# A hybrid DeltaNet / RWKV-7 / Mamba-2 layer on one core: a list scheduler inside the kernel orders every engine

## The chip, the core and the metric

The kernel runs on one core of a Trainium2 chip. The core has TensorE (PE, matrix products; its weight loads are shown apart as PEld), VectorE (DVE), ScalarE (ACT), GpSimd (POOL) and SyncE (SP), which each work through their own instructions in a fixed order, and DMA queues fed by SP and POOL. The metric is device microseconds (us) of one execution. The clock that TensorE is granted has two levels here, 2.4 GHz (shown as 1.00) and 1.2 GHz (0.50).

## What is computed

One residual layer over 16 meta frames and 1024 frames of width 1024. All three groups of heads read the same normalised input through one projection, and their outputs go through one output projection. Cut to what matters:

```python
hn = rms_norm(h, norm_pre)                       # (1040, 1024)
proj = einsum("bld,dp->blp", hn, w_in)           # 7832 columns, 61 tiles of 128 and 24 single ones
mixed = concat([
    gated_deltanet_group(p_a, ...),              # 6 heads of 128: conv, unit triangular solve per chunk, scan over chunks
    rwkv7_group(p_b, ...),                       # 8 heads of 64: token shift, low-rank decay, the same kind of solve and scan
    mamba2_group(p_c, ...)])                     # 12 heads of 64 in 4 groups: conv, chunked state-space scan
out = einsum("blm,md->bld", mixed, w_out)        # 2048 -> 1024
h = h + rms_norm(out, norm_post)
```

Each group multiplies its output by the silu of a gate, which is a tile of the projection of its own.

## The kernel before, in words

**Units.** The work is cut into twelve units: `unit_a` for each DeltaNet head (a0 to a5), `unit_b` for each pair of RWKV heads (b0 to b3), `unit_c` for each half of the Mamba heads (c0, c1), and at the end `unit_o`, the output projection. Each is a Python generator that writes instructions and yields at the points where it may be interrupted. `PLAN` gives the order in which units begin.

**Projections.** `proj` (L156) computes one 128-column tile of the input projection for all 1040 frames: in three pieces of about 350 frames, each 24 matmuls into one bank of PSUM (tile `pj`). Input and weights are split into a high and a low part in fp32r (`hh`, `hl` and the two halves of `w`), and for each of 8 blocks of the contraction three products are added: high weight by high input, high weight by low input, low weight by high input. `weights` (L142) brings a tile: SP loads it to `raw`, ACT writes the negated high part and the high part, and a DMA that POOL issues adds the raw weights to the negated part, which leaves the low part. 61 tiles make 4,392 matmuls. The output projection (tile `po`) has 768 more with 512 columns each, in the same fp32r form.

**Scans.** Everything else on PE (transposes, solves, the recurrences) is in plain fp32 with operands of 128, 64, 32 or 16 rows and columns; one such product stands in the trace as two matmul records. The solves of 32-blocks (`solve32`) run on DVE. A recurrence is a chain over chunks of PE, then DVE or ACT, then PE.

**Order.** `schedule` (L171) keeps a clock of its own from rough costs (`Meter`, L79): whenever the estimated time of a unit's next scan step has come, the step is written, otherwise the next products of a projection are ("fill"); a step counts as ready a margin after the last (`LATE`, `PIPE`, `SLOW`, and corrections to `lag`). Priorities (`PRI`, `EVA`, `CALM`) then let the framework's own scheduler move instructions. Units share two sets of PSUM banks ("lanes"); a third unit that scans shares a lane with another. 26 slots of SBUF (`NS`) are given to units by `safe`, so that a unit begins only when all can end. Projections that a unit needs late (its value, query and gate tiles) are put into a queue with a due time (`later`, `DUES`).

Of the kernel before, what the change touches and what calls it, by code (L numbers as in the profile page):

```python
# [7 lines left out]

# [6 lines left out]
F32 = mybir.dt.float32  # L15
# [6 lines left out]
D = 1024  # L22
KT = 8
# [5 lines left out]
FULL = ((0, 348), (348, 694), (694, 1040))  # L29
REAL = ((16, 358), (358, 700), (700, 1040))  # L30
# [12 lines left out]
XP = 500  # L43
# [6 lines left out]
SLOW = 1.0  # L50

PEAK = {"a": 7, "b": 12, "c": 14, "o": 24}
# [26 lines left out]
class Meter:  # L79


    def __init__(self, trunk, engine, fixed, each):
        self.trunk, self.engine, self.fixed, self.each = trunk, engine, fixed, each

    def __getattr__(self, name):
        op = getattr(self.engine, name)

        def call(out, *args, **kw):
            n = int(np.prod(out.shape[1:]))
            if name == "matmul":  # L90
                self.trunk.pe += n / 2400 if args[0].dtype == F32R else max(n, args[0].shape[-1]) / 600
            elif name == "transpose":
                self.trunk.pe += n / 1200
            elif not self.trunk.aside:
                self.trunk.lag += self.fixed + n * self.each
            return op(out, *args, **kw)  # L96

        return call


class Trunk:
    def __init__(self, tc, a):
        self.tc, self.nc, self.a = tc, tc.nc, a
        self.lane, self.pe, self.lag, self.aside = 0, 0.0, 0.0, False
        self.fetched, self.prefetch = {}, lambda i: None
        nc = tc.nc
        self.engines = tuple(Meter(self, e, f, n) for e, f, n in (
            (nc.vector, 0.25, 1 / 960), (nc.scalar, 0.3, 1 / 1200), (nc.tensor, 0, 0), (nc.gpsimd, 0.3, 1 / 500), (nc.sync, DMA, 0)))

    @contextmanager  # L110
    def off(self):

        self.aside = True
        yield
        self.aside = False
# [12 lines left out]
    def tmp2(self, name):  # L128
        return self.sm.tile([128, 2, 128], F32, tag="t2", name=name, bufs=1)
# [12 lines left out]
    def weights(self, i):  # L142
        nc = self.nc
        out = []
        for h in range(2):
            w = self.wp.tile([128, 2, 4, 128], F32R, tag="w", name=f"w{i}_{h}", bufs=NW)
            src = self.a["wt"][i][:, 4 * h: 4 * h + 4, :]
            raw = self.wp.tile([128, 4, 128], F32, tag="raw", name=f"wr{i}_{h}", bufs=NR)
# [7 lines left out]
    def proj(self, i, pieces, evac, halo=0):  # L156

        w = self.fetched.pop(i, None) or self.weights(i)
        for n, (a, b) in enumerate(pieces):
            a0 = max(a - halo, 0)  # L160
            p = self.pp.tile([128, 512], F32, tag="proj", name=f"pj{i}_{n}")
            for kt in range(KT):
                for m, (x, h) in enumerate(((0, self.hh), (0, self.hl), (1, self.hh))):
                    self.engines[2].matmul(p[:, : b - a0], w[kt // 4][:, x, kt % 4, :], h[:, kt, a0:b],
                                           start=(kt == 0 and m == 0), stop=(kt == KT - 1 and m == 2))
                    yield
            with self.tc.high_priority(EVA):
                evac(p, a, b, a - a0)
            if n == 0:
                self.prefetch(i)  # L170
# [33 lines left out]
    def setup(self):  # L204
# [15 lines left out]
        pk = cp.tile([128, sum(n for _, n in PACK)], F32, tag="pack", name="pack")  # L220
# [23 lines left out]
        for cc in XG:  # L244
# [5 lines left out]
            with self.tc.high_priority(XP):  # L250
# [116 lines left out]

    def unit_a(self, h):
# [34 lines left out]
        for cc, p in transposed(k, "akT", groups):  # L403
# [6 lines left out]
            yield PIPE  # L410
# [13 lines left out]
        for gi, cc in enumerate(groups):  # L424
# [7 lines left out]
            yield PIPE  # L432
# [12 lines left out]
        asked = self.later(h, self.conv(h, self.ctap_a[:, h, :], q, pieces=REAL), DUES[1])  # L445
        lb = self.one([128, 32, 32], f"alb{h}")
# [4 lines left out]
        yield 0.0  # L451
# [11 lines left out]
        for cc, p in transposed(v_, "avT", groups):  # L463
# [3 lines left out]
            yield PIPE  # L467
        yield from self.wait(asked)
        for cc, p in transposed(q, "aqT", groups[:2]):
# [3 lines left out]
            yield PIPE  # L473
        v.tensor_scalar(ss[:, 9:], ss[:, 9:], EPS, None, ADD)
        self.rsqrt(rs[:, 9:], ss[:, 9:], "a_q")
        self.lag = 0.0
        for gi, cc in enumerate(groups[:2]):
# [6 lines left out]
            yield PIPE  # L484
        yield 7
# [891 lines left out]
```

## Time and profile before

| | us |
|---|---|
| median of 3 runs | 1493.49 |
| lowest and highest | 1492.66, 1499.25 |
| the profiled execution | 1497.37 |
| its span, first to last instruction | 1495.2 |
| mean granted clock of TensorE in it (a share, 1 is full) | 0.956 |

The span is what the trace shows; the profiled execution's own time is 2.2 us longer, and 3.9 us above the median of the runs. PE is shown busy for 1439.9 us of the span, but its busy time overlaps from one matmul to the next, so the starts of successive matmuls are what tells how long each took.

### The profile page before, as it was taken

The numbers are of one execution on the slowest core, as the hardware profiler recorded it, in microseconds if no ns is written. First come the engines' busy times: TensorE is split into PE (matmuls) and PEld (weight loads), VectorE is DVE, ScalarE is ACT, GpSimd is POOL, SyncE is SP. The second block draws the span as 40 slices with busy tenths as digits, with TensorE's granted clock in tenths as the row PEclk, the third lists the DMA queues.
The fourth block names the chain that finished last, engine by engine and source line by source line (L and its number), as shares of the span: only waits on it lengthen the run. The fifth ranks groups of instructions, "written<-read, shape, count | busy, mean of one in ns | idle before, by whom it ended". The sixth has DMA issues, their size and how long they took to land.

```text
span 1495.2 us, 26098 instructions
## 1 busy us (share of the span) xinstructions
PE 1439.9 (96%) x9657; PEld 1274.6 (85%) x9657; DVE 954.8 (64%) x2688; ACT 707.2 (47%) x1936; POOL 173.4 (12%) x227
## 2 busy tenths in 40 slices
PE   5999999999999999999999999999999999999897
PEld 4999888888888789989888899889999988678686
DVE  6549485376768347869735787546588867542573
ACT  6455361345444364344746543544577255532530
POOL 2111000000001011111101111001132100200100
PEclk9999898799999799999979999889999999899999
DMA  7344332123223222434322244114534322553851
GB/s 225 87 114 85 81 61 58 43 62 93 51 46 75 67 71 72 116 65 103 76 86 57 62 85 96 29 43 99 118 97 105 71 58 59 171 162 89 259 191 57
DMA packets 120449, 136.28 MB, mean 91 GB/s; under 512 B 39867, under 2 KB 72379, under 8 KB 120323
## 3 DMA queue, kind: packets, MB, share of 16 engines
q1 hardware_dynamic: 102755, 102.64, 23.2%
q0 software_dynamic: 17568, 31.99, 12.7%
q8 instruction: 76, 1.25, 0.3%
q14 instruction: 50, 0.41, 0.1%
HBM read 116.99 MB, written 17.60 MB: 90 GB/s over the span
## 4 chain that ended last, share of the span: by engine, by line
PE 76%; issue 6%; DVE 6%; ACT 6%; DMA 5%; POOL 1%; SPq 0%; DVEq 0%; ACTq 0%; POOLq 0%
PE pj L96 41%; PE po L96 6%; PE bsi L96 5%; PE am L96 3%; PE bgr L96 2%; PE bu L96 2%; PE bm L96 1%; PE aops L96 1%; PE cdg L96 1%; PE ads L96 1%; PE bd L96 1%; PE av L96 1%; PE aks L96 1%; ACT buv L96 1%; DVE s_tmp L96 1%
## 5 line engine op out<-in xcount | busy, mean ns | idle before, releaser
L96 PE MATMUL pj<-hh,w 128*128 128x350 f32 (+8 forms) x2928 | 780.4, 340 | 4.5 <-DMA w<-in_wt_dram 2.7
L96 PEld LDWEIGHTS pj<-hh,w 128*128 128x128 f32 x2928 | 520.4, 193 | 19.4 <-DMA w<-in_wt_dram 2.9
L96 PE MATMUL pj<-hl,w 128*128 128x350 f32 (+8 forms) x1464 | 495.8, 339 | 0.0
L96 PEld LDWEIGHTS pj<-hl,w 128*128 128x128 f32 x1464 | 283.3, 193 | 6.1 <-issue 0.9
L152 POOL DMA_DIRECT2D w<-in_wt_dram x122 | 106.1, 870 | 903.5 <-ACT w L150 676.1
L150 ACT ACTIVATE w<-wr 128x512 fp32r<-128x512 f32 x122 | 76.6, 628 | 62.4 <-PE pj L96 61.2
L96 PE MATMUL po<-ow,omw 128*128 128x512 f32 x408 | 95.7, 395 | 4.1 <-ACT omw L1066 3.7
L96 PEld LDWEIGHTS po<-ow,omw 128*128 128x128 f32 x408 | 77.2, 191 | 22.6 <-ACT omw L1066 5.2
L96 PE MATMUL po<-ow,ome 128*128 128x512 f32 x360 | 92.0, 404 | 2.6 <-ACT ome L1066 1.2
L96 PEld LDWEIGHTS po<-ow,ome 128*128 128x128 f32 x360 | 67.8, 192 | 18.1 <-POOL ow L1049 2.1
L151 ACT CAST w<-wr 128x512 fp32r<-128x512 f32 x122 | 74.3, 609 | 0.1
L96 DVE TENSOR_TENSOR buv<-bu,b_ib 64x128 f32<-64x128 f32 x68 | 19.1, 281 | 81.2 <-PE bu L96 81.2
L96 PE MATMUL bsi<-buv,bgm 64*64 64x64 f32 (+1 forms) x528 | 62.1, 240 | 0.0
L96 DVE TENSOR_TENSOR alb<-alb,s_tmp 33x30 f32<-33x30 f32 (+9 forms) x180 | 56.7, 315 | 3.2 <-POOL alb L96 2.1
L96 DVE TENSOR_TENSOR s_tmp<-alb 33x30 f32<-33x30 f32 (+9 forms) x180 | 57.7, 320 | 1.1
L96 PEld LDWEIGHTS bsi<-buv,bgm 64*64 64x64 f32 (+1 forms) x528 | 42.6, 140 | 17.7 <-issue 3.2
L96 DVE SCALAR_TENSOR_TENSOR b_s<-bd,b_wc,b_s 64x64 f32<-64x64 f32 x120 | 33.9, 282 | 27.2 <-PE bd L96 23.1
L830 ACT COPY by<-bsi 64x128 f32<-64x128 f32 x64 | 16.8, 262 | 70.1 <-PE bsi L96 69.3
L96 ACT COPY b_x<-bsi 64x128 f32<-64x128 f32 x68 | 17.5, 258 | 62.7 <-PE bsi L96 62.4
L183 DVE SCALAR_TENSOR_TENSOR cbc<-pj,pack,cbc 128x346 f32<-128x346 f32 (+4 forms) x72 | 40.3, 567 | 9.8 <-ACT cbc L180 9.2
L1067 DVE TENSOR_TENSOR ome<-omre,ome 128x512 fp32r<-128x512 f32 (+2 forms) x40 | 22.9, 605 | 34.1 <-ACT ome L1066 34.0
L96 PE MATMUL bgr<-bar,bbk 64*128 64x128 f32 x272 | 42.4, 328 | 0.4 <-DVE bgm L96 0.4
(325 smaller groups left out, 2456.5 us busy)
## 6 DMA issues: line engine op xcount, KB each, us to landing
wr<-in_wt_dram SPq DMA_DIRECT2D x122, 256.0 KB, 3.4
w<-in_wt_dram POOLq DMA_DIRECT2D x122, 256.0 KB, 4.9
or<-in_w_out_dram SPq DMA_DIRECT2D x32, 256.0 KB, 4.2
omrw<-d_mix SPq DMA_DIRECT2D x32, 256.0 KB, 4.6
clt<-d_cs SPq DMA_DIRECT2D x24, 256.0 KB, 4.9
omre<-d_mix SPq DMA_DIRECT2D x24, 256.0 KB, 2.6
btw<-d_tw SPq DMA_DIRECT2D x8, 544.0 KB
x<-in_x_dram SPq DMA_DIRECT2D x8, 512.0 KB, 7.5
```

The source lines that it names most:

```text
L96: return op(out, *args, **kw)
L150: nc.scalar.activation(w[:, 1], raw, AF.Copy, scale=-1.0)
L151: nc.scalar.copy(w[:, 0], raw)
L152: nc.gpsimd.dma_start(w[:, 1], src, accum_op=ADD)
L183: nc.vector.scalar_tensor_tensor(acc[:, a + z: b], p[:, o + z - s: o + b - a - s], cw[:, 3 - s: 4 - s], acc[:, a + z: b], MUL, ADD)
L830: nc.scalar.copy(yt[hs[(c - 1) % 2], (c - 1) // 2, :], pq[64:128, 0:128])
L1067: nc.vector.tensor_tensor(t[:, 1], raw, t[:, 0].bitcast(F32), SUB)
```

## The change

The framework's ordering is replaced: each operation is recorded (`Scribe.write`) with the operations that it depends on and an estimate of its duration, and `schedule` emits, over all engines, whichever recorded instruction can start first, and ties each engine to that order. On PE it prefers a projection's matmul until 1.0 us of them have run (`BURST`), then emits the scan products that are ready, and keeps on while another becomes ready within 0.25 us (`JOIN`), first those of the same output tile. A decaying measure of the array's recent work (`heat`) forces projections when it is below `COLD`. Besides:

- within a piece of a projection, the 16 products with the high weights come first and the 8 with the low weights last; the next tile's weights are asked for after three matmuls of the first piece, before at its end
- gate tiles of `unit_a` and `unit_c` are computed in two pieces of 512 columns in place of three of 342
- the gates of a4 and a5 (`SOON`) are queued before the solve, in a slot more, in place of after it
- `PLAN` is another order; two units at most hold a lane, and a third waits with its scan
- `unit_o` loads one weight ahead in place of three, and each row block's final scaling is a task of its own

```diff
-LOOK, LATE, EVAC, DMA = 0.05, 0.3, 2.0, 5.0
-NOA = 3
-PIPE = 0.5
+NOA = 1
-PRI, EVA, CALM = 300, 700, 1500
+BURST, JOIN = 1.0, 0.25
+COOL, COLD = 3.0, 0.36
+LESS = {"scan": 0.0, "ev": 0.3, "ld": 0.5, "calm": 1.0, "off": 0.4}
+AHEAD = 8
-PLAN = "a0 b0 b1 b2 c0 b3 a1 a2 a3 c1 a4 a5"
+PLAN = "a0 b0 b1 a1 c0 b2 a2 c1 b3 a3 a4 a5"
+SOON = (4, 5)
...
-            for kt in range(KT):
-                for m, (x, h) in enumerate(((0, self.hh), (0, self.hl), (1, self.hh))):
-                    self.engines[2].matmul(p[:, : b - a0], w[kt // 4][:, x, kt % 4, :], h[:, kt, a0:b],
-                                           start=(kt == 0 and m == 0), stop=(kt == KT - 1 and m == 2))
-                    yield
+            steps = [(kt, 0, h) for kt in range(KT) for h in (self.hh, self.hl)] + [(kt, 1, self.hh) for kt in range(KT)]
+            for j, (kt, x, h) in enumerate(steps):
+                if n == 0 and j == 3:
+                    self.prefetch(i)
+                with self.of(cls="pj"):
+                    self.engines[2].matmul(p[:, : b - a0], w[kt // 4][:, x, kt % 4, :], h[:, kt, a0:b],
+                                           start=(j == 0), stop=(j == len(steps) - 1))
+                yield
...
+        return self.later(18 + h, self.proj(18 + h, HALF, gate), DUES[2])
...
+    def emit(self, i, start):
+        r = i.go()
...
+            self.tc.add_manual_dep(ins, was, mybir.DependencyInfo(mybir.DependencyClass.NoSync, mybir.DependencyReason.DATA), reason="order")
...
+                    if s["kind"] != "scan" or s["drop"] and s["want"] is None or s["task"].q["PE"] or s["task"].n > AHEAD:
+                        continue
+                    if s["on"] and not s["on"]["done"] or not safe(s):
+                        continue
+                    if s["lane"] is None:
+                        open_ = [g for g in range(len(GB)) if all(o["lane"] != g for o in active)]
+                        if not open_:
+                            continue
+                        s["lane"] = open_[0]
...
+                if e == "PE":
+                    now = self.free["PE"]
+                    pj = min((h for h in heads if h[2].cls == "pj"), key=lambda h: h[0], default=None)
+                    sc = [h for h in heads if h[2].cls != "pj"]
+                    sc = min(sc, key=lambda h: (h[0] > now + 0.02 if h[2].out == last else 1, h[0]), default=None)
+                    if pj is None or sc is None:
+                        pick = sc or pj
+                    elif heat * float(np.exp((self.seen_at - now) / COOL)) < COLD:
+                        pick = pj
+                    elif round_:
+                        pick = sc if sc[0] <= max(now + JOIN, pj[0]) else pj
+                    else:
+                        pick = sc if since >= BURST and sc[0] <= max(now + 0.03, pj[0]) or sc[0] < pj[0] - 0.3 else pj
+                else:
+                    first = min(h[0] for h in heads)
+                    pick = min((h for h in heads if h[0] <= first + 0.05), key=lambda h: h[1] + LESS[h[2].cls])
+                if best is None or pick[0] < best[0]:
+                    best = pick
```

## Rows read from the trace of the kernel before

**Rows 1.** The page: span, busy time by engine, and TensorE's granted clock in 40 slices.

```profile
span 1495.2 us, 26098 instructions
PE 1439.9 (96%) x9657; PEld 1274.6 (85%) x9657; DVE 954.8 (64%) x2688; ACT 707.2 (47%) x1936; POOL 173.4 (12%) x227
PEclk9999898799999799999979999889999999899999
```

**Rows 2.** Stretches: length; busy (count) of PE, PEld, DVE, ACT, POOL; granted clock; DMA.

```profile
104.80:108.20 3.40, 3.40 (x12) 3.40 (x12) 0.95 (x3) 2.07 (x3) 0.00 (x0) 0.50 0.12 39
...
248.10:282.30 34.20, 34.20 (x174) 25.87 (x175) 10.01 (x22) 6.08 (x17) 0.88 (x1) 0.50 0.07 12
493.90:511.00 17.10, 17.10 (x134) 14.34 (x130) 4.22 (x10) 5.72 (x15) 0.87 (x1) 0.50 0.16 45
760.10:777.20 17.10, 17.10 (x84) 13.59 (x82) 3.39 (x11) 5.28 (x15) 0.86 (x1) 0.50 0.15 32
...
1391.60:1395.00 3.40, 3.40 (x9) 2.61 (x9) 1.87 (x4) 1.94 (x4) 1.50 (x1) 0.50 0.96 280
```

**Rows 3.** The same view for tile pj alone: projections in two of these stretches.

```profile
248.10:282.30 34.20, 5.20 (x13) 3.43 (x14) 0.00 (x0) 0.00 (x0) 0.50 0.07 12
...
760.10:777.20 17.10, 6.20 (x13) 3.71 (x14) 0.00 (x0) 0.00 (x0) 0.50 0.15 32
```

**Rows 4.** PE in order of time at the lower clock: start, length of the group, operation.

```profile
264.86 0.47 PE L96 MATMUL bsi<-buv,bgm 64*64 64x64 f32 x2
265.26 0.80 PE L96 MATMUL bgr<-bar,bbk 64*128 64x128 f32 x4
265.99 0.47 PE L96 MATMUL bsi<-buv,bgm 64*64 64x64 f32 x2
```

**Rows 5.** PE in order of time at the full clock: one round between projections.

```profile
401.23 0.48 PE L96 MATMUL pj<-hh,w 128*128 128x346 f32 x2
401.55 0.32 PE L96 MATMUL pj<-hl,w 128*128 128x346 f32 x1
401.71 0.38 PE L96 MATMUL bd<-buv,bbt 128*128 128x128 f32 x2
402.02 0.45 PE L96 MATMUL bsi<-buv,bgm 128*64 128x64 f32 x4
402.39 0.58 PE L96 MATMUL pj<-hh,w 128*128 128x346 f32 x2
402.82 0.32 PE L96 MATMUL pj<-hl,w 128*128 128x346 f32 x1
```

**Rows 6.** PE in order of time: products of one form in a row.

```profile
1002.87 0.39 PE L96 MATMUL aops<-a_s,aq 128*128 128x128 f32 x2
1003.10 0.39 PE L96 MATMUL aops<-a_vn,aup 128*128 128x128 f32 x2
...
1202.58 1.14 PE L96 MATMUL am<-add,alo 64*64 64x64 f32 x16
```

**Rows 7.** PE in order of time: first and last round of the twelve units.

```profile
76.44 1.03 PE L96 MATMUL akT<-pack,ak 128*128 128x128 f32 x8
...
1321.58 1.09 PE L96 MATMUL aoT<-pack,avt 128*128 128x128 f32 x8 [1.52 <-DVE avt L96]
```

**Rows 8.** PE in order of time near the end: products with 512 columns.

```profile
1483.83 3.33 PE L96 MATMUL po<-ow,omw 128*128 128x512 f32 x14
```

**Rows 9.** Waits of PE: who waited for whom, us in total, times, longest.

```profile
PE xT L260 <- DVE x L255: 10.9, 1, 10.9
PE xT L260 <- DVE hl L264: 7.3, 5, 2.6
PE po L96 <- ACT omw L1066: 3.7, 1, 3.7
...
PE bvT L96 <- ACT buv L96: 2.2, 4, 1.1
...
PE aops L96 <- ACT avt L96: 1.6, 1, 1.6
```

More of the change, by code (lines that the diff above doesn't have):

```diff
@@ L76, in nt, with __init__ @@
     return NM if c == 0 else 128
-class Meter:
-    def __init__(self, trunk, engine, fixed, each):
-        self.trunk, self.engine, self.fixed, self.each = trunk, engine, fixed, each
+class Instr:
+    __slots__ = ("go", "eng", "deps", "cls", "step", "extra", "mode", "work", "lock", "took", "start", "done", "task", "out")
+class Task:
+    def __init__(self, name):
+        self.name, self.q = name, {e: [] for e in ENGINES}
+        self.n = 0
+ENGINES = ("PE", "ACT", "DVE", "POOL", "SP")
+SEES = {"PE": 0.055, "ACT": 0.035, "DVE": 0.035, "POOL": 0.075, "SP": 0.027}
@@ L85, in __getattr__, with __init__ @@
+class Scribe:
+    def __init__(self, trunk, key, engine):
+        self.trunk, self.key, self.engine = trunk, key, engine
     def __getattr__(self, name):
-        op = getattr(self.engine, name)
+        op, t = getattr(self.engine, name), self.trunk
+        if not t.writing:
+            return op
         def call(out, *args, **kw):
[L89 to L96, printed above, removed]
@@ L98, in __getattr__, with __init__, tile @@
-        return call
+            t.write(self.key, name, op, out, args, kw)
+        return call
+class Engines:
+    def __init__(self, trunk, nc):
+        self.vector, self.scalar, self.tensor = (Scribe(trunk, k, e) for k, e in (("DVE", nc.vector), ("ACT", nc.scalar), ("PE", nc.tensor)))
+        self.gpsimd, self.sync = Scribe(trunk, "POOL", nc.gpsimd), Scribe(trunk, "SP", nc.sync)
+class Pool:
+    def __init__(self, trunk, pool, bufs):
+        self.trunk, self.pool, self.bufs, self.made = trunk, pool, bufs, defaultdict(list)
+    def tile(self, shape, dt, tag, name, bufs=None):
+        t = self.pool.tile(shape, dt, tag=tag, name=name, **({} if bufs is None else {"bufs": bufs}))
+        if self.trunk.writing and tag != "s":
+            made, n = self.made[tag], bufs or self.bufs
+            key = t.tensor.name
+            if len(made) >= n:
+                old = made[-n]
+                self.trunk.born[key] = [a[2] for a in self.trunk.seen.get(old, ())]
+            made.append(key)
+        return t
@@ L110, in off, with of @@
-    @contextmanager
-    def off(self):
-        self.aside = True
-        yield
-        self.aside = False
+        self.nc = nc = Engines(self, tc.nc)
+        self.engines = (nc.vector, nc.scalar, nc.tensor, nc.gpsimd, nc.sync)
+        self.seen, self.born, self.task, self.cls = {}, {}, None, "scan"
+        self.before, self.free = {}, {e: 0.0 for e in ENGINES}
+        self.array, self.bus, self.held = None, 0.0, {"DVE": 0.0, "POOL": 0.0}
+    @contextmanager
+    def of(self, task=None, cls=None):
+        was = self.task, self.cls
+        self.task, self.cls = task or was[0], cls or was[1]
+        yield
+        self.task, self.cls = was
@@ new lines, in ready, with begins @@
+    def ready(self, i):
+        if i.start is None:
+            t = 0.0
+            for d in i.deps:
+                if d.done is None:
+                    return None
+                if not d.eng == i.eng == "PE":
+                    t = max(t, d.done + SEES[i.eng])
+            i.start = t
+        return i.start
+    def begins(self, i, t):
+        t = max(t, self.free[i.eng])
+        if i.lock:
+            other = self.held["POOL" if i.eng == "DVE" else "DVE"]
+            if t < other:
+                t = other + 0.02
+        return t
@@ new lines, in schedule @@
+        while True:
+            advance()
+            best = None
+            for e in ENGINES:
+                heads = []
+                for t in self.tasks:
+                    if t.q[e]:
+                        i = t.q[e][0]
+                        r = self.ready(i)
+                        if r is not None:
+                            heads.append((self.begins(i, r), r, i))
+                if not heads:
+                    continue
+                if e == "PE":
[9 more added lines that the diff above has]
+                        pick = sc if sc[0] <= max(now + JOIN, pj[0]) else pj
+                    else:
+                        pick = sc if since >= BURST and sc[0] <= max(now + 0.03, pj[0]) or sc[0] < pj[0] - 0.3 else pj
+                else:
+                    first = min(h[0] for h in heads)
+                    pick = min((h for h in heads if h[0] <= first + 0.05), key=lambda h: h[1] + LESS[h[2].cls])
+                if best is None or pick[0] < best[0]:
+                    best = pick
+            if best is None:
+                left = [t.name for t in self.tasks if t.n]
+                if left or units or active or self.queue or fill or out:
+                    raise ValueError(f"no part fits: {left} {units} {[(s['name'], s['has'], s['want'], s['drop'], s['kind']) for s in active]}")
+                break
+            start, _, i = best
+            if i.eng == "PE":
+                was = self.free["PE"]
+                if i.cls == "pj":
+                    since = since + i.step if not round_ else i.step
+                    round_ = False
+                else:
+                    round_ = True
+                last = i.out
+                heat = heat * float(np.exp((self.seen_at - start) / COOL)) + i.work / COOL
+                self.seen_at = start
+            self.emit(i, start)
+            self.tasks = [t for t in self.tasks if t.n or t is self.loader or t is self.mixer or any(t is s["task"] for s in active) or fill and (
+                t is fill.get("task") or fill.get("unit") and t is fill["unit"]["task"]) or planned and planned.get("unit") and t is planned["unit"]["task"]]
```

405 lines of the change are left out of this document (280 added, 125 removed).

## The prediction

> **What bounds the kernel now.** I read the page first. PE is shown busy 96% of the span, DVE 64%, ACT 47% [rows 1], so the question is what PE's time is made of. The waits of PE are next: the two largest are 18.2 us at the start, before any projection, and the others are single events of 0.5 to 4 us [rows 9]. So PE hardly ever waits for another engine, and a better order can't win much by removing waits. What it can win is that the same matmuls take less time each.
>
> PE's busy times overlap, so I took from the order in time the distance from each start to the next. A projection's product with 346 columns takes 0.16 us, also where `hh` and `hl` alternate [rows 5]; a product with 512 columns takes (3.33 - 0.38) / 13 = 0.227 us, where 0.38 is my reading of the last one's own length [rows 8]. An fp32 record of 128 by 128 takes 0.115 us (two from 1002.87 to 1003.10), one of 64 by 64 about 0.06 us ((1.14 - 0.2) / 15) [rows 6]. With such bare prices for every form, all matmuls together come to about 1267 us. From the first to the last start there are 1476 us. The 209 us between are what the change can reach, and two things make up most of it.
>
> The first is the clock. Of the stretches after the setup in which the granted clock is 0.50, the first begins at 104.8 us and the last at 1391.6; there are ten, of 126.5 us together [rows 2]. In nine of them PE is busy without a gap: 34.20 of 34.20 us in the longest. It isn't idling that they share, but what runs: 13 of 174 matmuls in that longest one are projections, 13 of 84 in another [rows 3]; the rest are small products. Everything takes about twice as long there: two 64-wide products and the change to the next form take 0.40 us [rows 4], and four with theirs 0.37 at the full clock [rows 5]. That fits a clock that falls with the amount of work in the array. The last stretch is another kind: it follows a wait of 3.7 us for `omw` [rows 2, 9].
>
> The second is changes of form. In one round at the full clock, bd takes 0.31 us where two bare records take 0.23, bsi 0.37 where four 64-wide ones take 0.24 [rows 6], and the two projections behind them 0.43 where they cost 0.32 [rows 5]: 0.08 + 0.13 + 0.11, so about 0.1 us a change. From the first to the last round I count 559 rounds of other matmuls, the first and the last of which are shown [rows 7], with 470 further changes of form inside them, and 558 runs of projections between, of which 405 have six products or fewer, that is under 1.0 us.
>
> **The change part by part.**
>
> *The clock (heat, COLD).* With little recent work in the array the scheduler now puts a projection ahead of a ready scan step. The projections aren't new work, only moved, and such stretches had one open: some of its products run in them [rows 3]. If the clock stayed up throughout, the 126.5 us would shrink to 63, a gain of 63; if it did nothing, 0. I take 46: nearer to the full gain because the condition that I read from rows 2 and 3 is the one that the rule acts on, and less than it because the wait at 1391 isn't touched, because slots can leave no projection open, and because each one put in costs changes of form.
>
> *Rounds (BURST, JOIN, outputs kept together).* Runs under 1.0 us are no longer chosen, unless the projection itself isn't ready. Where two units scan at once, their steps then meet in one round; where one scans alone, the round only comes later. Two rounds that meet save one change, 0.1 us. Bounds: none of the 405 meets, 0; all do, 41 us. I take half, 21, since mostly two units scan. In rounds, the rule of the last output tile keeps records of one tile together, where rows 4 show bsi and bgr cutting into each other every two to four records; of 470 changes I let 50 go, 5 us (bounds 0 and 15). Together 26.
>
> *Gate tiles in two pieces.* Three pieces of 342 are 72 products of 0.157 us (the 346-column price less 4 columns), 11.3 us; two of 512 are 48 of 0.227, 10.9 us. Over 12 tiles that is 5 us, and fewer evacuations on ACT and DVE, which have room. The Trainium skill ("TensorE: Matmul & The Clock Gate", Back-to-back issue gap) puts a product at columns / 2.4 GHz plus 2.5 ns: by that 10.44 and 10.36 us, an estimate of 1 us over all twelve, since the columns are the same. The rows are 12 ns above it for either width, so the number of products does count here, and the rows decide.
>
> *Low weights last, weights asked for earlier.* The low half is ready after the negated copy and POOL's DMA; now it is needed 16 products (2.5 us) into a tile. But PE's waits for `w` are below those of rows 9 but one of 2.7 us. Taken at 0; bounds 0 and 3. The cover is that weights of the next tile are fetched during a whole tile; if a tile runs with no scans between, it lasts 72 x 0.16 = 11.5 us, still enough.
>
> *Gates early, the other plan, one output weight ahead, the tail.* The same products in another place. Fetching two output weights later can make PE wait at the start of `unit_o`, and the row block's final scaling is off its neighbours' queue; I set 0, with 5 us either way, the size of the single waits there [rows 9].
>
> *New waits.* Before, a scan step was placed with a margin behind its estimated time; now it is placed when the estimate says that its input lands, and PE, DVE and ACT take it in that order, so an estimate that is short makes PE stand, and the projections queued behind it too. Nothing in this trace shows how good the estimates are. Single waits for ACT or DVE in rows 9 are 0.5 (bvT, 2.2 in 4) to 1.6 us (aops). None: 0. If every fifth of some 400 rounds waited 0.5 us: 40. I take 10, as rows 9 show few waits where rough costs with margins served, and finer costs without margins should miss by less than 0.5 us and not often.
>
> Sum: -46 - 26 - 5 + 10 = -67. From 1495.2 that leaves a span of 1428; with 2.2 us around it an execution of 1430; and since the profiled execution is 3.9 above the median, **1426 us** as the median of runs.
>
> **The rivals.**
>
> *The clock doesn't follow the mix.* If it falls for another reason, the 46 is lost: 1426 + 46 = 1472. The Trainium skill speaks for this (same page, HAM oscillation): it tells of clocks that fall in gaps, while PE waits for data. By that rule, mixing helps nothing where PE never idled, and the time would be these 1472. The trace doesn't agree: the clock fell in stretches with no idle time at all [rows 2].
>
> *Two lanes become the bound (slower).* Before, a third unit could scan in a shared lane. Now a unit holds its lane from its first scan step to its end, its waits for gates included, and BURST delays its steps. From first to last own matmul the twelve units last 152 to 290 us and 2648 together. On two lanes that is 1324 us; from 76.4 us on [rows 7] to 1400, and behind it the 173 us from the last unit's last matmul to the end: 1573. They needed 1245 before, which is 2.1 lanes. It decides once the units stay over 208 us in the mean, against 221 now; below, PE's own work is longer. Against it: these lengths are mostly queueing behind projections and three-way sharing and not the chains' own latency. If units shrink only halfway to 208, the time is still 1535.
>
> *The gains go into waits.* If estimates miss often (40 us) and projections run out so that the clock gives 20, rounds 15 and gates 5, nothing is left: about 1493.
>
> *All of it works.* The clock's 60, 35 from rounds, 5 from gates, no new waits: 1393.
>
> **How the numbers follow.** My forecast holds 0.47, all of it works 0.2, the clock rival 0.13, gains lost to waits 0.07, the lanes 0.13. A measurement here can tell about 0.5% from no change, 7.5 us: faster is below 1486, slower above 1501. The first three are faster, 0.80; then 0.07 the same and 0.13 slower. The forecast alone is 1395 to 1465: down by 14 if the clock gives 60, by 10 without new waits and by 7 with a few more rounds that meet; up by 21 if the clock gives 25, by 15 with waits of 25 and by 3 for the tail. For 8 in 10 I go down to 1385, below the case in which all works, and up to 1488, past the clock rival; the same and the slower cases are left out.
>
> **What would show it.** Right: the granted clock at full after the setup but for short stretches (mean above 0.98), fewer than 450 rounds and hardly a run of projections under six products except where weights are late, gate tiles as 512-wide products (576 records), PE's waits under 60 us in all, and the last unit's last matmul near 1255 us. Wrong: stretches at 0.50 with projections mixed in (the clock rival); long stretches with no projection at all and waits of PE on DVE or ACT in them, with units that begin late (lanes); many waits of 0.2 to 0.5 us spread over all forms (estimates).

## The result, and the profile after

The kernel became slower. The median of four runs is 1536.03 us (1534.85 to 1552.75), beside 1496.12 us for four runs of the kernel before on the same chip: a ratio of 1.0299, with a 95% interval of 1.0233 to 1.0366. Predicted were 1426 us, with a range that ended at 1488. Medians in this document are of all executions, while ratios leave out the slower ones, among them two of variants below that took 2237.62 and 5685.41 us, at a mean granted clock of 0.594 and 0.222.

The page of the changed kernel gives span, busy time by engine and the granted clock, as [rows 1] do for the kernel before:

```profile
span 1534.1 us, 25489 instructions
PE 1433.8 (93%) x9369; PEld 1257.5 (82%) x9369; DVE 972.7 (63%) x2674; ACT 704.6 (46%) x1916; POOL 173.3 (11%) x227
PEclk9899999999799999999997999999697997899999
```

PE's busy time hardly fell and its share of the span went from 96% to 93%: PE now stands. The waits of PE, which answer to [rows 9] (who waited for whom, us in total, times, longest):

```profile
PE xT L466 <- DVE x L461: 10.8, 1, 10.8
PE po L210 <- ACT ome L210: 6.4, 1, 6.4
PE xT L466 <- DVE hl L470: 6.1, 5, 2.5
PE am L210 <- DVE add L210: 6.1, 6, 3.1
PE p L210 <- ACT p L210: 5.5, 1, 5.5
PE bbon L210 <- ACT buv L210: 4.8, 5, 2.5
PE bm L210 <- DVE bdd L210: 4.8, 1, 4.8
```

Behind the two at the start the largest was one of 3.7 us before; now five shown here pass 4 us in all, and scan tiles (bbon, bm, am) are among them.

**Where the time went.** I took the prediction's own account again: for every matmul the distance from its start to the next one's, split into the bare price of its form (from the kernel before, at the full clock), the idle time of PE ahead of the next, and the rest, at either clock. "Idle" is time in which no matmul is shown on PE. The sums, from the first start to the last, in us:

| | before | after | change | predicted |
|---|---|---|---|---|
| bare prices (gate tiles) | 1266.7 | 1263.2 | -3.5 | -5 |
| PE idle after its first matmul (new waits) | 36.4 | 80.1 | +43.7 | +10 |
| rest at the lower clock | 74.2 | 77.0 | +2.8 | -46 |
| rest at the full clock (changes of form) | 98.6 | 93.2 | -5.4 | -26 |
| sum | 1475.9 | 1513.5 | +37.6 | -67 |

The spans differ by 38.9, so the account holds nearly all. Waits of PE over 0.2 us went from 38 to 87, by 42.3 us in all: 11.1 us of the growth is in waits up to 0.5 us (49 where there were 19), 11.7 in those up to 1.5 us, and 19.5 in those above, which went from 18.4 us to 37.9.

**What PE waited for.** Two places in order of time, ACT's and DVE's queue and then PE (in brackets the idle time ahead, and what ended it):

```profile
198.35 0.63 ACT L210 ACTIVATE w<-wr 128x512 fp32r<-128x512 f32 x1 [1.92 <-DMA wr<-in_wt_dram]
...
200.56 1.07 ACT L210 COPY buv<-bvT 64x128 f32<-64x128 f32 x4
...
201.68 0.70 PE L210 MATMUL bbon<-bat,pack 128*128 128x512 f32 x1 [2.51 <-ACT buv L210]
...
380.19 0.18 DVE L210 TENSOR_TENSOR s_tmp<-alb 33x30 f32<-33x30 f32 x1 [5.33 <-DMA alb<-d_m]
...
382.36 0.79 DVE L210 STREAM_TRANSPOSE bdd<-bgm 32x288 f32<-32x288 f32 x2
...
382.87 1.16 PE L210 MATMUL bm<-bdd,bgm 32*32 32x32 f32 x18 [4.79 <-DVE bdd L210]
```

In the first, ACT's queue holds a weight's cast that waits for its load; behind it, in the order that the scheduler fixed, stand three more casts and the copies of `buv` that PE needs next. In the second, DVE waits 5.33 us for `alb` to come back through DRAM, `bdd` is behind it, and PE stands 4.79 us for `bdd`. The list of waits names ACT and DVE; in these two places what came late were transfers, in another unit's work. The groups by line, after, show the same (busy, mean ns, then idle time ahead and what ended it):

```profile
L210 ACT ACTIVATE w<-wr 128x512 fp32r<-128x512 f32 x120 | 75.4, 628 | 25.0 <-DMA wr<-in_wt_dram 23.2
...
L210 DVE TENSOR_TENSOR s_tmp<-alb 33x30 f32<-33x30 f32 (+9 forms) x180 | 58.6, 325 | 19.8 <-DMA alb<-d_m 16.3
...
L210 DVE TENSOR_TENSOR s_tmp<-blb 68x30 f32<-68x30 f32 (+14 forms) x120 | 40.0, 333 | 22.8 <-DMA blb<-d_l 20.3
```

and in the kernel before:

```profile
L96 DVE TENSOR_TENSOR s_tmp<-alb 33x30 f32<-33x30 f32 (+9 forms) x180 | 57.7, 320 | 1.1
```

The plan's landing times are short beside these. It puts a weight's load at 4.0 us, more than the median of 3.4 on the page of the kernel before; the page after gives 4.6 (the last column below), from the 21 of 122 loads whose landing the trace tells, two of which took over 7. For `clt` the plan has 4.2; 6.6 is the median of two landings. (Two forecasts below say 4.2 and 4.3; the kernel's own values are these.)

```profile
wr<-in_wt_dram SPq DMA_DIRECT2D x122, 256.0 KB, 4.6
...
clt<-d_cs SPq DMA_DIRECT2D x24, 256.0 KB, 6.6
```

**The clock.** Stretches at the lower clock, as in [rows 2]:

```profile
381.90:399.00 17.10, 16.13 (x150) 14.74 (x151) 12.27 (x35) 6.08 (x14) 1.81 (x3) 0.50 0.22 62
822.20:839.30 17.10, 17.10 (x84) 14.98 (x81) 4.11 (x9) 5.49 (x12) 0.91 (x2) 0.50 0.00 1
1068.00:1098.70 30.70, 26.59 (x116) 20.83 (x117) 9.11 (x40) 14.38 (x55) 5.05 (x6) 0.50 0.21 45
1266.00:1283.10 17.10, 16.81 (x136) 14.40 (x137) 11.86 (x30) 6.56 (x15) 1.76 (x2) 0.50 0.07 9
```

The first begins at the wait of 4.79 us shown above, the last at one of 3.1 us for `am`; the second has no gap, as before. I called a stretch one "with waits" where the waits of PE that end between 5 us before and 3 us after its beginning add up to 1.5 us; the one at the very end of the span is left out. Before, 3 of 10 stretches and 27 of 126 us were such; after, 9 of 14 and 102 of 154. Those without waits halved, from 99 to 51 us (to 41 if the one from 1317.2 is left out, which begins inside the wait of 6.4 us for `ome` but before the last 4 us of it). So what was won in the one kind was lost again in the other. That the two meet by chance is unlikely: the same test, put at every half microsecond, holds at 8% of the points after and 3% before. But it is no law: of 10 single waits over 1.5 us behind the first 20 us, 6 have such a stretch beside them.

### The profile page after: what moved, and what is told of

Its sections match the earlier page's. It is cut to its first block, busy times and chain, and to the rows that moved or that the text cites. A ratio compares the mean times of both kernels' runs of the same rounds, so it can differ in the third digit from the quotient of the medians.

```text
span 1534.1 us, 25489 instructions
## 1 busy us (share of the span) xinstructions
PE 1433.8 (93%) x9369; PEld 1257.5 (82%) x9369; DVE 972.7 (63%) x2674; ACT 704.6 (46%) x1916; POOL 173.3 (11%) x227
## 4 chain that ended last, share of the span: by engine, by line
PE 58%; DVE 19%; ACT 9%; DMA 7%; issue 5%; SPq 2%; POOL 1%; DVEq 0%; ACTq 0%; POOLq 0%
PE pj L210 26%; PE po L210 9%; PE bsi L210 4%; PE am L210 2%; DVE s_tmp L210 2%; DVE cx L210 2%; PE bgr L210 2%; PE bu L210 2%; DMA wr<-in_wt_dram 2%; DVE blb L210 1%; DVE clt L210 1%; SPq L210 1%; PE bd L210 1%; PE bm L210 1%; ACT w L210 1%
## 5 line engine op out<-in xcount | busy, mean ns | idle before, releaser
L210 PE MATMUL pj<-hh,w 128*128 128x350 f32 (+7 forms) x2688 | 735.0, 349 | 1.6 <-DMA w<-in_wt_dram 1.6
L210 PEld LDWEIGHTS pj<-hh,w 128*128 128x128 f32 x2688 | 485.0, 194 | 26.7 <-issue 2.2
L210 PE MATMUL pj<-hl,w 128*128 128x350 f32 (+7 forms) x1344 | 468.9, 352 | 0.0
L210 PEld LDWEIGHTS pj<-hl,w 128*128 128x128 f32 x1344 | 264.1, 197 | 13.1 <-issue 1.3
L210 PE MATMUL po<-ow,omw 128*128 128x512 f32 x432 | 98.6, 390 | 0.6 <-ACT po L210 0.6
L210 PEld LDWEIGHTS po<-ow,omw 128*128 128x128 f32 x432 | 80.9, 188 | 18.1 <-ACT po L210 1.3
L210 PE MATMUL po<-ow,ome 128*128 128x512 f32 x336 | 86.1, 405 | 6.4 <-ACT ome L210 6.4
L210 ACT ACTIVATE w<-wr 128x512 fp32r<-128x512 f32 x120 | 75.4, 628 | 25.0 <-DMA wr<-in_wt_dram 23.2
L210 PEld LDWEIGHTS po<-ow,ome 128*128 128x128 f32 x336 | 62.1, 192 | 19.2 <-ACT ome L210 6.9
L210 DVE TENSOR_TENSOR s_tmp<-alb 33x30 f32<-33x30 f32 (+9 forms) x180 | 58.6, 325 | 19.8 <-DMA alb<-d_m 16.3
L210 DVE TENSOR_TENSOR s_tmp<-blb 68x30 f32<-68x30 f32 (+14 forms) x120 | 40.0, 333 | 22.8 <-DMA blb<-d_l 20.3
L210 DVE SCALAR_TENSOR_TENSOR a_s<-a_s,sc_etot,ads 128x128 f32<-128x128 f32 x42 | 14.4, 343 | 44.6 <-PE ads L210 44.4
L210 DVE TENSOR_TENSOR blb<-blb,s_tmp 68x30 f32<-68x30 f32 (+14 forms) x120 | 39.1, 326 | 5.0 <-POOL blb L210 2.2
```

The lines of the kernel that those rows point to most:

```text
L210: i.go, i.eng, i.cls, i.task, i.done, i.start = (lambda: op(out, *args, **kw)), key, self.cls, self.task, None, None
```

## The experiments

Two theories run through them. One: the plan's times are short, PE stands in a fixed order, and the clock falls behind its waits. The rival: the waits are a side effect, and what costs is in the new order itself, the clock rule, the rounds or the plan. The scheduler rewrites the whole order on any change of a number, so each kernel is also another order. Account of each, in the terms of the table above, as differences to the changed kernel in us (idle, lower clock, full clock): this is worked out once here and used below. Each row is one execution, and executions of one of these kernels differ by 6 to 23 us, so a term of a few us says little.

| | idle | lower clock | full clock | sum |
|---|---|---|---|---|
| PE's margin 0.355 | +6.4 | -31.0 | -3.2 | -27.8 |
| PE's margin 0.555 | +9.5 | -30 | -9 | -29.1 |
| no clock rule | -0.4 | +18.6 | -3.4 | +13.2 |
| all transfers 2 us later | -11.0 | -16.4 | +2.5 | -24.9 |
| weights alone 3 us later | -9.6 | -15.0 | +5.9 | -18.7 |
| other transfers 2 us later | -10.8 | -36.7 | +6.8 | -40.6 |
| the same without clock rule | -2.6 | +9.1 | -5.6 | +0.8 |
| no rounds | -9.9 | +150.0 | +46.7 | +185.1 |
| the old plan | +17.3 | +5.9 | +5.1 | +28.3 |
| small corrections together | -14.0 | -12 | -5 | -30.8 |
| margin and other transfers | -15.4 | -35.7 | -9.2 | -60.3 |

(Where a sum differs by up to 1.7 from its terms, other bare prices make it up.)

**A margin for PE.** An input counts as ready for PE 0.3 us later.

```diff
-SEES = {"PE": 0.055, "ACT": 0.035, "DVE": 0.035, "POOL": 0.075, "SP": 0.027}
+SEES = {"PE": 0.355, "ACT": 0.035, "DVE": 0.035, "POOL": 0.075, "SP": 0.027}
```

> The changed kernel, but PE's planner sees every input 0.3 us later (0.355 in place of 0.055 us after the writer's end), so a scan product is placed with a margin, as the kernel before did. Theory 1 (PE stands because products are placed at the instant that the plan gives, and real ACT, DVE and DMA are later): PE's idle time falls from 90.8 us to between 45 and 65, and the time by 15 to 35 us, to 1500 to 1520, although the kernel's own plan ends 11 us later. Theory 2 (PE stands because no projection is open: slots and lanes): idle time stays within 10 us of 90 and the time is 1536 to 1550.

1507.94 us (1497.74 to 1513.72), 1.0098 of the kernel before [1.0054, 1.0142]. Two thirds of the loss came back (2.0 of 3.0%), but PE's idle time, which theory 1 saw at 45 to 65 us, rose by 6.4; by the account nearly all of the gain is in the clock. ACT's waits for `wr` and DVE's for `alb`, 23.2 and 16.3 us in the changed kernel, are longer here:

```profile
L210 ACT ACTIVATE w<-wr 128x512 fp32r<-128x512 f32 x120 | 75.2, 626 | 38.4 <-DMA wr<-in_wt_dram 34.3
...
L210 DVE TENSOR_TENSOR s_tmp<-alb 33x30 f32<-33x30 f32 (+9 forms) x180 | 57.4, 319 | 22.4 <-DMA alb<-d_m 19.0
```

So two thirds of the loss can come back with these waits untouched.

**The clock rule off.**

```diff
-COOL, COLD = 3.0, 0.36
+COOL, COLD = 3.0, 0.0
```

> The changed kernel with COLD = 0, so that low recent work of the array no longer forces a projection. Theory A (the rule holds the clock up, and without it things would be worse): the time at the lower clock after the setup grows from 150 us to 200 or more, and the execution by 20 us or more. Theory B (the rule hardly acts on the clock, which falls after waits that the plan doesn't know): the time at the lower clock changes by less than 30 us and the execution by less than 10.

1553.07 us (1549.52 to 1555.67), 1.0386 [1.0323, 1.0450], and a mean clock of 0.931 to 0.939 in four executions, for 0.942 to 0.952. That is 0.8% above the changed kernel, 13 us: between the two forecasts, and the intervals of the two times overlap. The clock speaks for the rule; the pair of runs with later transfers, below, is clear of noise.

**Transfers later in the plan.**

```diff
-            i.done = max(start + i.took, self.bus + 1.3)
+            i.done = max(start + i.took, self.bus + 1.3) + 2.0
```

> The changed kernel with 2 us more in the planner's landing time of every SyncE transfer, and nothing else. If the late inputs are late because of transfers (clt took 6.6 us where the plan has 4.3), PE's idle time falls by 20 us or more and the time by 10 to 30. If they are late for ACT and DVE, idle time falls by less than 10 and the time stays within 10 us of 1536 or rises by the 20 us by which the kernel's own plan grows.

1517.76 us (1505.11 to 1527.43), 1.0147 [1.0052, 1.0241]. No work is added, only the plan's belief changes, and half of the loss comes back. PE's idle time fell by 11 us, again between the two forecasts.

**Gate pieces and low weights alone, in the kernel before.**

```diff
+HALF = ((16, 528), (528, 1040))
-        gated = self.later(18 + h, self.proj(18 + h, REAL, gate), DUES[2])
+        gated = self.later(18 + h, self.proj(18 + h, HALF, gate), DUES[2])
...
+            steps = [(kt, 0, h) for kt in range(KT) for h in (self.hh, self.hl)] + [(kt, 1, self.hh) for kt in range(KT)]
```

> The kernel before with two parts of the change alone: gate tiles of two heads' groups in two pieces of 512 columns, and the products with the low weights last in each piece. By the prediction's terms 5 us from the gates and 0 to 3 from the low weights: ratio to before 0.994 to 0.997, and 288 projection matmuls fewer. A rival: the evacuations of the wider pieces come later and hold the bank longer, ratio 1.00 or above.

1492.93 us, 0.9960 [0.9924, 0.9995] of the kernel before: 6 us, beside the 5 predicted for the gates with nothing for the low weights. Its one trace is 7.7 us shorter in the account: 3.5 from bare prices, the rest from 13.1 us more idle and 18.6 less at the lower clock, so only the 3.5 can be read from the products.

**The weights' loads alone, 3 us later.**

```diff
+            i.done = max(start + i.took, self.bus + 1.3) + (3.0 if i.out.startswith("wr") else 0.0)
```

> The changed kernel with 3 us more in the planner's landing time of the input projection's raw weights alone (the profile has a median of 4.6 us and a tenth above 7; the plan has 4.2). If PE's new waits come from ACT standing at a cast of weights that haven't landed, with scan copies queued behind it, ACT's waits for wr fall from 23 us to under 8, PE's idle time falls by 15 us or more, and the time by 15 to 25. If these waits of ACT cost PE nothing, idle time stays within 8 us of 90 and the time within 10 of 1536.

1518.17 us (1505.09 to 1527.86), 1.0162 [1.0115, 1.0208]: 1.4 of the 3.0% come back. PE's idle time fell by 9.6 us where 15 or more were expected. ACT's idle time for weights fell as meant (the same group as above, in this kernel, with forms kept apart):

```profile
L210 ACT ACTIVATE w<-wr 128x512 fp32r<-128x512 f32 x120 | 75.1, 626 | 7.9 <-DMA wr<-in_wt_dram 7.7
```

**All other transfers of SP, 2 us later.**

```diff
+            i.done = max(start + i.took, self.bus + 1.3) + (0.0 if i.out.startswith("wr") else 2.0)
```

> The changed kernel with 2 us more for every SyncE transfer but those weights: the round trips of the solves through memory, the decays, the operands of the output projection. If PE's new waits come from DVE standing at the first step of a solve whose block hasn't landed (36 us of DVE's waits in the changed kernel), these fall below 15 us and the time falls by 10 to 20; if not, the time is within 10 us of 1536 or above by the 23 us that the plan grows. The runs with 2 us on all transfers took 18 us off, so this and the weights' run should share that between them if the effects add.

1496.94 us (1490.6 to 1506.11), 0.9992 [0.9953, 1.0031]: the whole loss is gone. DVE's groups by line in this kernel:

```profile
L210 DVE TENSOR_TENSOR s_tmp<-alb 33x30 f32<-33x30 f32 (+9 forms) x180 | 57.7, 321 | 3.9
...
L210 DVE TENSOR_TENSOR s_tmp<-blb 68x30 f32<-68x30 f32 (+14 forms) x120 | 39.0, 325 | 25.6 <-DMA blb<-d_l 23.6
```

The wait for `alb` is gone (19.8 before this edit), that for `blb` is not. Time at the lower clock halved, over the whole span from 159 to 79 us; most of the gain is there. ACT waits longer for `wr` than in the changed kernel, 31.9 us for 23.2. This and the run before don't add up to the one that moves all transfers.

**A margin of 0.5 us.**

```diff
-SEES = {"PE": 0.055, "ACT": 0.035, "DVE": 0.035, "POOL": 0.075, "SP": 0.027}
+SEES = {"PE": 0.555, "ACT": 0.035, "DVE": 0.035, "POOL": 0.075, "SP": 0.027}
```

> The margin of PE's inputs at 0.5 us in place of 0.3. If a margin helps because small misses of the plan no longer make PE stand, a larger one helps a little more or as much: 1495 to 1510, and the time at the lower clock 70 to 100 us. If it helped by chance of one order, the time goes back towards 1520 to 1540.

1508.48 us, 1.0073 [1.0031, 1.0115]: what 0.355 gave. More margin doesn't shorten the time further.

**No rounds.** Scan steps are written as soon as they are ready, the new scheduler otherwise as it is.

```diff
-BURST, JOIN = 1.0, 0.25
+BURST, JOIN = 0.0, 0.0
```

> The changed kernel with BURST and JOIN at 0: a scan product is placed as soon as the plan has it ready, without a least run of projections before. If changes of form cost PE what the prediction took (0.1 us each), the rounds grow from 403 to 600 or more and the time rises by 20 us or more above 1536 (the kernel's own plan rises by 88). If rounds are worth nothing on the chip, the time is within 10 us of 1536.

1711.68 us (1704.84 to 1721.4), 1.138 [1.1286, 1.1473], with 825 rounds in place of 403. The page's granted clock:

```profile
PEclk9899799999655999996799799999877996979999
```

The mean is 0.889. Of the 185 us, 150 are at the lower clock and 47 at the full one. By the 0.1 us a change of the prediction, 422 more rounds cost 42 us, about the latter; the former I had not priced at all. In this kernel 341 us at the lower clock lie in stretches without waits: here the clock fell while PE was busy. The longest:

```profile
445.80:555.00 109.20, 108.83 (x436) 70.08 (x437) 19.61 (x45) 20.66 (x50) 3.69 (x5) 0.50 0.06 14
```

Of its 436 matmuls 145 are projections, so it is not filled with small products alone; that the frequent change between the two does it is argued, since this kernel is another order too.

**Other transfers later, and the clock rule off.** Two edits from above together.

```diff
-COOL, COLD = 3.0, 0.36
+COOL, COLD = 3.0, 0.0
-            i.done = max(start + i.took, self.bus + 1.3)
+            i.done = max(start + i.took, self.bus + 1.3) + (0.0 if i.out.startswith("wr") else 2.0)
```

> The version with 2 us more for the round trips, and COLD = 0 as well. Theory: the rule does hold the clock up in dense stretches of scan products, which only shows when long waits of PE no longer take the clock down. Then the stretches at the lower clock that follow no wait come back, the time at the lower clock rises from 75 us after the setup to 120 or more, and the execution from 1497 to 1515 or above. Rival: without these waits the rule isn't needed; time within 8 us of 1497.

1535.59 us, 1.0226 [1.0158, 1.0294], 2.3% or 35 us above the kernel with the transfers alone (41 by the account of the two traces). The stretches without waits went from 14 to 79 us. Two of the windows at the lower clock:

```profile
191.70:212.20 20.50, 20.50 (x129) 17.82 (x128) 9.44 (x29) 5.62 (x15) 0.00 (x0) 0.50 0.35 79
461.30:471.50 10.20, 10.20 (x86) 9.05 (x86) 3.03 (x9) 3.38 (x10) 0.00 (x0) 0.50 0.01 2
```

PE is busy for 20.50 of 20.50 us; projections are 36 of the 129 matmuls in the first window and 7 of the 86 in the second. With later transfers the rule is worth 35 us, clear of noise.

**The plan of the kernel before, in the changed kernel.**

```diff
-PLAN = "a0 b0 b1 a1 c0 b2 a2 c1 b3 a3 a4 a5"
+PLAN = "a0 b0 b1 b2 c0 b3 a1 a2 a3 c1 a4 a5"
```

> The changed kernel with the order of units of the kernel before. If the new order is part of what made it slower, 1505 to 1525; if it is a gain that is hidden (the kernel's own plan ends 28 us later with the old order, and stretches without any projection grow from 140 to 202 us in it), 1555 to 1590.

1568.14 us, 1.0461 [1.0407, 1.0515]: the new order isn't the cause, with this scheduler the old one costs 1.6% more, 24 us (28 by the account).

**Small corrections together.**

```diff
-SEES = {"PE": 0.055, "ACT": 0.035, "DVE": 0.035, "POOL": 0.075, "SP": 0.027}
+SEES = {"PE": 0.155, "ACT": 0.035, "DVE": 0.035, "POOL": 0.075, "SP": 0.027}
-COOL, COLD = 3.0, 0.36
+COOL, COLD = 3.0, 0.33
-            i.done = max(start + i.took, self.bus + 1.3)
+            i.done = max(start + i.took, self.bus + 1.3) + (2.0 if i.out.startswith("wr") else 1.5)
```

> The corrections together: 0.1 us of margin for PE's inputs, 2 us more for the raw weights, 1.5 us for all other transfers, and the clock rule a little weaker (COLD 0.33). If the misses of the estimates are the cause and the corrections add, PE's idle time falls below 75 us, the time at the lower clock after the setup stays below 90, and the time is 1465 to 1485, under both kernels. If they don't add (each only reshuffles one order), 1490 to 1520.

1506.39 us, 1.0030 [0.9985, 1.0075]. It did not add what the single edits gave.

**Margin and other transfers.**

```diff
-SEES = {"PE": 0.055, "ACT": 0.035, "DVE": 0.035, "POOL": 0.075, "SP": 0.027}
+SEES = {"PE": 0.355, "ACT": 0.035, "DVE": 0.035, "POOL": 0.075, "SP": 0.027}
-COOL, COLD = 3.0, 0.36
+COOL, COLD = 3.0, 0.33
-            i.done = max(start + i.took, self.bus + 1.3)
+            i.done = max(start + i.took, self.bus + 1.3) + (0.0 if i.out.startswith("wr") else 2.5)
```

> 0.3 us of margin for PE's inputs, 2.5 us more for all transfers but the raw weights, COLD 0.33. If the two corrections that each gained most alone (28 us and 39 us) add, 1465 to 1480; if both repair the same waits, 1490 to 1505.

**1472.61 us** (1471.35 to 1478.29), 0.9832 [0.9791, 0.9873]: faster than both kernels, by 1.7% and, by the two ratios, 4.5%, with the scheduler's structure untouched. Three values differ at once, so the gain isn't shared out among them. Its page:

```profile
span 1473.9 us, 25450 instructions
PE 1388.8 (94%) x9369; PEld 1227.4 (83%) x9369; DVE 970.0 (66%) x2674; ACT 701.9 (48%) x1916; POOL 173.2 (12%) x227
PEclk9899999999999999999999999997999999799999
```

Its largest waits of PE behind the start, and its longest stretch at the lower clock:

```profile
PE po L210 <- ACT ome L210: 5.8, 1, 5.8
PE p L210 <- ACT p L210: 5.5, 1, 5.5
PE ads L210 <- ACT a_vn L210: 5.4, 5, 3.5
PE cdg L210 <- DVE cst L210: 3.8, 2, 3.6
```

```profile
1014.50:1038.40 23.90, 19.95 (x150) 15.91 (x146) 6.24 (x29) 15.13 (x55) 5.81 (x8) 0.50 0.15 47
```

In that stretch no projection runs at all: the rule has nothing to put in. The weights keep their short landing time here, and ACT waits longer for them than in the changed kernel:

```profile
L210 ACT ACTIVATE w<-wr 128x512 fp32r<-128x512 f32 x120 | 75.4, 628 | 37.2 <-DMA wr<-in_wt_dram 29.9
```

## Why the prediction was wrong

**The steps that failed are "New waits" and, with it, the clock taken as independent of it.** The sum came out 105 us too low: 49 us of that are the clock's, 34 the waits', 21 the rounds'. For the waits I took 10 us between bounds of 0 and 40; 43.7 were measured, past the upper bound. I argued from the few waits in [rows 9] that finer costs without margins would miss by under 0.5 us. That was the wrong row to argue from: it shows what PE waited for under an order with margins, in which 0.3 to 2 us stood behind each step. The many waits of 0.2 to 0.5 us that I had named as a sign are there, but only 11.1 us of the growth is in them, and 19.5 of 42.3 in those over 1.5 us. I priced PE's estimates and not the transfers', and not that ACT and DVE take their order too, so that a late load of one unit stops the copy of another.

How much of the loss is due to late transfers stays open. That late landings stop PE is seen in the two places above, and the runs that change nothing but the plan's landing times win back 1.4 to 3.1%, with the named waits of ACT for `wr` cut to a third in one and of DVE for `alb` gone in another. But PE's idle time fell by only 10 to 11 of the 43.7 us in them, and the margin alone won 2.0% with both named waits longer than in the changed kernel. What is shown is that the time hangs on the plan's estimates; all these gains lie mostly at the lower clock.

**The clock: -46 predicted, +2.8 measured.** The rule does what I said: without it 35 us are lost in the kernel with later transfers, 13 in the changed one (where the intervals overlap), and the stretches without waits halved. What I left out is that a stretch at the lower clock can stand beside a wait, too. I had the case before me, the wait for `omw` and the 3.4 us behind it [rows 2, 9], and set it aside as "another kind". Two more of the ten were of it, 17.1 us behind a wait for `bdd` (the stretch from 493.9 in [rows 2]) and 6.9 us around one for `avt`:

```profile
491.39 0.75 PE L96 MATMUL bm<-bdd,bgm 32*32 32x32 f32 x18 [2.80 <-DVE bdd L779]
...
941.00:947.90 6.90, 6.01 (x22) 5.84 (x23) 3.68 (x9) 2.10 (x8) 0.00 (x0) 0.51 0.00 0
```

The two terms aren't independent: the 75 us more of stretches with waits (27 to 102), which take twice the time, are about 37 of the 49 us that the clock term is off, if all of them are put down to waits; in the longest of them, 30.7 us from 1068.0, only 13 of 116 matmuls are projections, so the rule may have had little to put in. No run takes the waits away alone. Where the time came back, both kinds fell: from 102 us with waits and 51 without to 82 and 10 with PE's margin, 61 and 14 with the other transfers later, and 55 and 27 in the fastest kernel. The Trainium skill ("TensorE: Matmul & The Clock Gate", HAM oscillation) tells of clocks that fall in gaps while PE waits for data. The trace after agrees with it in 9 of 14 stretches, and in four of the other five not (the fifth, from 1317.2, begins inside a wait). I let it stand only as a rival, because most of the stretches before had no idle time. Both happen, and I should have priced that case for every wait that the change adds.

**Rounds: -26 predicted, -5.4 measured.** Rounds fell from 559 to 400 (403 with three ahead of the units' first) and runs of at most six products from 405 of 558 to 91 of 399, better than the forecast of under 450 rounds. At the full clock, the change from a projection to a scan step fell from 29.7 to 15.2 us, and what lies between successive projections from 46.1 to 40.5. But the way back went from -9.0 to -5.5, and inside the rounds changes of form rose from 19.7 to 24.9 us and steps of one form from 12.0 to 18.2. So the price was mis-sized: to go into a round and out of it cost (29.7 - 9.0) / 559, about 0.04 us in the mean and not the 0.1 that I read from one round, and the 11 us saved there came back inside the rounds. The records of one tile were kept together more often: 487 changes inside rounds beside 470 look like none of it, but a round that joins another makes a change inside out of a beginning, and both together fell from 1,029 to 890. In the run without rounds the price was 0.11 us a round (47 us for 422), so no one price holds. What rose inside the rounds goes with PE's margin: by the same account of the other kernels these two terms, 43 us here and 32 before, are 42 to 46 us where the margin is the changed kernel's and the rounds stay, 39 with 0.155 us, 28 and 32 with 0.355 and 23 with 0.555. Waits too short to stand as idle time, since the record of one matmul overlaps the next, would do this; no row shows them singly. The rounds' larger effect is one that I had not connected with them: without them the lower clock takes 150 us more.

**Gate tiles: -5 predicted, -3.5 in the bare prices**, with 4,104 products of the input projection where there were 4,392; the run of these parts alone gives 6, its interval 1 to 11. **Low weights last** shows nothing against my 0. **Gates early, plan, tail**: 0 taken; the new plan is worth 24 us under this scheduler, which my 0 did not hold; what it is worth under the scheduler before wasn't tried. In the tail, the wait for `ome` is 6.4 us where `omw` had 3.7 [rows 9]. It and the 5.5 us of `p` at the start are still there, at 5.8 and 5.5, in the fastest kernel.

**The rivals.** The slower side came true, though two lanes were not its bound. The twelve units last 2364 us together, 197 in the mean, below the 208 from which two lanes would decide, and less than the 221 before. They end later all the same (the last scan's matmul at 1390.4 us where I forecast 1255). On two lanes 2364 us fill 1182 of the 1308 us from the first to the last own matmul, so lanes were nine tenths taken; no kernel with a third lane was run, and their share in the delay is open. "The gains go into waits" named the mechanism and stopped at 40 us of waits, with 20 left from the clock. "The clock doesn't follow the mix" is refuted as the whole account: the clock fell for 341 us without waits in the run without rounds, and stretches without waits came back when the rule was taken away (14 to 79 us). The sign that I had set for it, projections mixed into the stretches, came too, but it was no sign. I had looked at two of ten stretches [rows 3], and in others projections were up to all of the matmuls. Tile pj alone, two stretches before and one after:

```profile
104.80:108.20 3.40, 3.40 (x12) 3.40 (x12) 0.55 (x1) 0.51 (x1) 0.50 0.12 39
...
493.90:511.00 17.10, 10.03 (x27) 7.60 (x28) 2.72 (x5) 1.54 (x3) 0.50 0.16 45
```

```profile
822.20:839.30 17.10, 11.66 (x35) 9.84 (x35) 3.55 (x7) 1.74 (x3) 0.50 0.00 1
```

What the stretches without waits share is rather what ran ahead of them: in the 4 us before each, 38 of 413 matmuls were projections in the kernel before and 24 of 245 after (the stretch from 1317.2 apart), where from the units' first matmul to their last it is half.

**What stays open.** The corrected kernel still has 28 us more idle time than the kernel before (64.7 beside 36.4). Its parts, 5.5 and 5.8 us at both ends and single waits of 1.5 to 3.6 us among them, weren't tried one by one. The stretch without an open projection (24 us in the fastest kernel, 30.7 with 13 products in the changed one) points to the slots or the units' start, untested. Each kernel is also a new order, so part of every difference, in the clock above all, may be that order's luck: corrections didn't add up twice.

## What to carry to other kernels

An order fixed over all engines is as good as its estimates: a late input stops whatever else stands behind it on ACT or DVE, and then PE. Here 2 to 3 us more on planned landing times, or 0.3 us of margin for PE, won 1.4 to 3.1% without any work taken away. Try each by itself: to add 2 us to all transfers gave less than to leave the weights out. When a change adds waits, price each twice, for the idle time and for the time at the lower clock that may follow. And when a trace shows few waits, ask which margins made them few before taking them away.

## What the runs showed of the hardware

The granted clock fell in two ways: while PE was busy without a gap (20.50 of 20.50 us, 36 of 129 matmuls projections; 10.20 of 10.20 us, 7 of 86), after 4 us in which few of the matmuls were projections (38 of 413 in the kernel before), and beside single waits of 2 to 6 us, with 3.4 to 17.1 us at 0.50. Of the waits in the changed kernel, those of 2.5 us at 201.7 and 2.0 us at 359.2 had no such stretch. I had not expected the second kind to weigh as much as the first. The same 256 KB weight load landed in 3.4 us by the median before (20 landings that the trace tells) and in 4.6 after (21), with the same number of loads and bytes in another order: a landing time measured under one order did not hold under the next.
